# Two-layer hybrid encoder on one core: gates' products one stage ahead, strips and paired values in the recurrence, the logarithm's guard on VectorE

## The chip, the cores and the metric

One core of one Trainium2 chip runs the whole kernel. The metric is device time in microseconds of one launch, of which three runs are shown; a profile of one further execution goes with them. Engines: TensorE (PE; its weight loads are a row of their own, PEld), VectorE (DVE), ScalarE (ACT), GpSimd (POOL), and SyncE (SP), which issues all transfers here.

## What is computed

Batch 1, 512 tokens, width 1024, two layers, float32. Each layer adds three gated branches, then cross-attention over 256 memory tokens, then a SwiGLU of width 2816:

```python
h = _rmsnorm(x, g_mix[l])
(a_cq, a_ckv, a_kr, b_q, b_ff, b_fb, b_i, b_g,
 c_q, c_k, c_v, gate_a, gate_b, gate_c) = _split_cols(h @ w_in[l], IN_SPLITS)
y_a = _mla(...)          # latent attention, 8 heads
y_b = _hgrn2(...)        # bidirectional gated recurrence, 8 heads, 128 keys, 64 values
y_c = _window_gqa(...)   # attention within 128 tokens, 8 heads
merged = (sigmoid(gate_a) * (y_a @ w_br_a[l]) + sigmoid(gate_b) * (y_b @ w_br_b[l])
          + sigmoid(gate_c) * (y_c @ w_br_c[l]))
x = x + merged @ w_out[l]
x = x + _cross(_rmsnorm(x, g_x[l]), _rmsnorm(mem, g_mem[l]), ...)
x = x + _swiglu(_rmsnorm(x, g_ffn[l]), ...)
```

In the recurrence each direction has a forget gate f per key and token, `log f = log(max(f, TINY))`, decayed queries and keys, and a state; forward and backward outputs of a head are added.

## The kernel before, in words

Activations lie transposed, 128 features by 512 tokens a tile. Products of weights are made of float32r parts: every weight tile is split into a high part (ScalarE, L120) and a low part (VectorE, L121), and `mm3` issues three matmuls (high by high, high by low, low by high). Weights come as one stream of 764 units of 128x512, fetched by SP (L112) into five buffers, split three units ahead of their use; a unit is 4 blocks, so 12 matmuls of 512 columns. Operands that aren't split go to TensorE as plain float32 through `mm` (L151, which is the line of nearly all matmuls).

A layer goes through the recurrence (`hgrn`), latent attention (`mla`), windowed attention (`window`), the end of the merge, the output projection, cross-attention and the feed-forward part. A scheduler puts each engine's instructions into an order when the program is built; the Python order sets priorities. In `mla` and `window`, work of other branches is put between their steps as "fillers": the gates' products (`gates`, L513: 8 chunks of 128 features, 24 matmuls each), their sigmoid, which stays in a buffer, and the branch's output product (`out`, L525), two chunks of gates and then the two products they gate. Branch B fills `mla`, branch A fills `window`, and branch C mostly follows after it.

In `hgrn` the decay of head i+2 (`hgrn_decay`) is worked out while head i is at its scores. The decay takes the logarithm in two pieces, since the table's range doesn't hold it in one: f clamped from above by KNEE and below by TINY on GpSimd (L404), f clamped from below on VectorE (L405), two logarithms (L406, L407), and their sum on GpSimd (L408); then scans (L411 and on), the decayed queries and keys (L438, L439), and their level tables `lt` (L457). `hgrn_scores` makes a 512x512 matrix of scores of one head as 4x4 blocks of 128 tokens (keys on the partitions). The diagonal blocks come in pieces: a full 128x128 product forward into bank `bd` and one backward into bank `bb` (L469, L470), and over them 64x64 and 32x32 products from the level tables (L472 to L478). A mask selects (`copy_predicated`, L482), the two are added (L484) and split (L487, L488). The off-diagonal blocks fill three more banks (L490 to L502), each split too (L504). The values of one head are 4 x 3 matmuls of 128 columns by 512 (L367), of which 64 rows are kept. Values themselves are turned by `vturn` (L280) and split.

Of the kernel before, what the change touches and what calls it, by code (L numbers as in the profile page):

```python
# [48 lines left out]
def _consts():  # L49
# [21 lines left out]
    mb = same & (p[:, None] >= p[None, :])  # L71
# [4 lines left out]
class _K:  # L76
# [119 lines left out]
    def setup(self):  # L196
# [25 lines left out]
        self.zz = self.tl("zz", [P, 2, 4, P])  # L222
        nc.gpsimd.memset(self.zz, 0.0)
# [66 lines left out]
    def hgrn(self, l, x, xg, acc):  # L290
# [13 lines left out]
        def take_z(hd, zs):  # L304
# [27 lines left out]
        take_z(heads[1], [proj("f", 1), proj("b", 1)])  # L332
# [3 lines left out]
        a = self.hgrn_scores(heads[0])  # L336
        decay(heads[1])
        y = self.pairs4(4)
        for i in range(8):
            pr = i // 2  # L340
            if i > 0:
                a = self.hgrn_scores(heads[i])
            if i % 2 == 0:
                osb = self.t2()
                if 0 < i < 6:
                    values(pr + 1)
            else:
# [6 lines left out]
            if i < 6:  # L354
                take_z(heads[i + 2], [proj("f", i + 2), proj("b", i + 2)])
# [7 lines left out]
            ob = self.bank()  # L363
            vh, vl = vs[pr]
            for j in range(4):
                s = slice(j * T, (j + 1) * T)
                self.mm3(ob, (vh[:, j], vl[:, j]), (a[0][:, s], a[1][:, s]), j == 0, j == 3)  # L367
            hf = slice(64 * (i % 2), 64 * (i % 2) + 64)
            nc.scalar.activation(osb[hf], ob[hf], AF.Copy)
            if i % 2 == 1:  # L370
                sq = self.t2()
# [22 lines left out]
    def hgrn_decay(self, l, hd, d):  # L394
# [9 lines left out]
        nc.gpsimd.tensor_scalar(g, f, TINY, KNEE, op0=ALU.max, op1=ALU.min)  # L404
# [55 lines left out]
    def hgrn_scores(self, hd):  # L460
# [5 lines left out]
        bd, bb = self.bank([P, 4, P]), self.bank([P, 4, P])  # L466
        for j in range(4):
            js = slice(j * P, (j + 1) * P)
            one(bd[:, j], qk[:, 1, js], qk[:, 0, js])  # L469
            one(bb[:, j], qk[:, 3, js], qk[:, 2, js])  # L470
        for j in range(4):
            one(bd[0:64, j, 64:128], lf[:, 1, 1, 64 * j:64 * j + 64], lf[:, 1, 0, 64 * j:64 * j + 64])  # L472
            one(bd[64:128, j, 0:64], lr[:, 1, 1, 64 * j:64 * j + 64], lr[:, 1, 0, 64 * j:64 * j + 64])
            for i in range(2):
                a, b = 64 * i, 64 * i + 32
                ps = slice(64 * j + 32 * i, 64 * j + 32 * i + 32)
# [685 lines left out]
```

## Time and profile before

| | us |
|---|---|
| runs | 2447.57, 2450.2, 2451.07 (median 2450.2) |
| profiled execution, its own time | 2445.72 |
| its span (first to last instruction) | 2443.9 |
| TensorE busy, matmuls / weight loads | 2396.9 / 1966.2 |
| VectorE / ScalarE / GpSimd busy | 1503.9 / 1194.2 / 262.9 |
| bytes moved | 220.96 MB, 90 GB/s over the span |

Busy time of TensorE is that of matmuls that overlap one another; a float32 matmul stands as two records. A stage's idle time of TensorE is its length less its busy time. Times are us from the first instruction.

### The profile page before, as it was taken

To read this page: it belongs to the slowest core of one execution; us is meant where nothing else is said; L and a number is where in the kernel's file an instruction comes from. 1 tells how busy PE (TensorE), PEld (TensorE's weight loads), DVE (VectorE), ACT (ScalarE), POOL (GpSimd) and SP (SyncE) were. 2 spreads that over 40 slices of the span, in tenths; PEclk is the share of its full clock that TensorE was granted. 3 is DMA by queue.
4 is the path that set the end of the run, shared out by engine and by line. 5 is a ranking of instruction groups with operands and counts; after the bars stand their busy time and mean duration, and the time that the engine had idled before them with its cause. 6 is when DMAs were issued, how large, how long until landed. Compare 5 with 4: busy or idle time off the path is not lost.

```text
span 2443.9 us, 32499 instructions
## 1 busy us (share of the span) xinstructions
PE 2396.9 (98%) x11974; PEld 1966.2 (80%) x11974; DVE 1503.9 (62%) x2745; ACT 1194.2 (49%) x2169; POOL 262.9 (11%) x197
## 2 busy tenths in 40 slices
PE   8999999999999999999998999999999999999998
PEld 6788877788888888888877887877888888888886
DVE  8877766665565655355577786666656566553553
ACT  7666665555444533233466665654544444332332
POOL 2455300000000000000035452000000000000000
PEclk9999999999999999999999999999999999999999
DMA  4212222123442333333421212212324522333332
GB/s 141 61 57 70 82 70 66 62 82 107 151 139 86 91 96 95 99 95 99 127 77 61 70 61 74 74 57 71 90 84 148 147 87 82 96 95 99 96 98 75
DMA packets 119681, 220.96 MB, mean 90 GB/s; under 512 B 13281, under 2 KB 15585, under 8 KB 119137
## 3 DMA queue, kind: packets, MB, share of 16 engines
q1 hardware_dynamic: 119520, 218.88, 29.8%
q8 instruction: 94, 1.54, 0.3%
q14 instruction: 67, 0.54, 0.1%
HBM read 214.63 MB, written 4.19 MB: 90 GB/s over the span
## 4 chain that ended last, share of the span: by engine, by line
PE 85%; DVE 8%; ACT 3%; POOL 2%; issue 1%; DMA 1%; SPq 0%; DVEq 0%; ACTq 0%; POOLq 0%
PE ps L151 83%; POOL t L404 2%; DVE c L457 1%; PE ps L643 1%; DVE smx L411 1%; PE ps L784 1%; POOL t L408 1%; DVE c L439 1%; DVE t L411 1%; DVE wlo L121 1%; DVE c L181 0%; ACT whi L120 0%; DVE c L438 0%; DVE zz L482 0%; DMA c<-in_memT_dram 0%
## 5 line engine op out<-in xcount | busy, mean ns | idle before, releaser
L151 PE MATMUL ps<-c,whi 128*128 128x512 f32 (+1 forms) x5696 | 1734.7, 387 | 6.5 <-ACT whi L120 6.2
L151 PEld LDWEIGHTS ps<-c,whi 128*128 128x128 f32 x5696 | 1059.4, 188 | 232.8 <-issue 10.4
L151 PE MATMUL ps<-c,wlo 128*128 128x512 f32 (+1 forms) x2848 | 1098.4, 386 | 15.3 <-DVE wlo L121 15.2
L120 ACT ACTIVATE whi<-wraw 128x512 fp32r<-128x512 f32 x764 | 475.3, 630 | 858.1 <-PE ps L151 626.3
L121 DVE TENSOR_TENSOR wlo<-wraw,whi 128x512 fp32r<-128x512 f32 x764 | 521.0, 690 | 552.9 <-ACT whi L120 539.8
L151 PEld LDWEIGHTS ps<-c,wlo 128*128 128x128 f32 x2848 | 536.1, 188 | 127.3 <-DVE wlo L121 20.5
L151 PE MATMUL ps<-c,t 128*128 128x512 f32 (+6 forms) x1024 | 188.0, 393 | 4.0 <-DVE c L181 3.7
L404 POOL TENSOR_SCALAR t<-t 128x512 f32<-128x512 f32 x32 | 71.8, 2244 | 1067.4 <-ACT t L401 1065.9
L151 PEld LDWEIGHTS ps<-c,t 128*128 128x128 f32 (+2 forms) x1024 | 127.8, 176 | 48.0 <-issue 20.2
L457 POOL TENSOR_TENSOR c<-c,smx 128x256 f32<-128x256 f32 x128 | 144.9, 1161 | 73.8 <-DVE c L438 61.4
L982 DVE TENSOR_TENSOR t<-ps,t 128x512 f32<-128x512 f32 x112 | 76.3, 688 | 103.0 <-PE ps L151 103.0
L151 PE MATMUL ps<-c 128*32 128x32 f32 (+3 forms) x1280 | 110.6, 259 | 5.5 <-DVE c L439 5.5
L151 PEld LDWEIGHTS ps<-c 128*32 128x32 f32 (+2 forms) x1280 | 96.8, 151 | 21.9 <-DVE c L439 4.0
L181 DVE TENSOR_TENSOR c<-ps,c 128x512 fp32r<-128x512 f32 (+2 forms) x126 | 80.2, 650 | 23.7 <-ACT c L180 23.4
L180 ACT ACTIVATE c<-ps 128x512 fp32r<-128x512 f32 (+2 forms) x126 | 68.4, 565 | 43.9 <-PE ps L151 42.6
L964 DVE TENSOR_TENSOR c<-ps,c 128x512 f32<-128x512 f32 x64 | 44.2, 691 | 72.8 <-PE ps L151 72.8
L457 DVE TENSOR_TENSOR c<-c,smx 128x256 f32<-128x256 f32 x128 | 67.7, 587 | 0.3
L408 POOL TENSOR_TENSOR t<-t,t 128x512 f32<-128x512 f32 x32 | 45.1, 1409 | 86.7 <-ACT t L407 86.7
L181 DVE TENSOR_TENSOR c<-t,c 128x512 fp32r<-128x512 f32 (+1 forms) x84 | 51.9, 632 | 2.9 <-ACT c L180 2.9
L180 ACT ACTIVATE c<-t 128x512 fp32r<-128x512 f32 (+1 forms) x84 | 48.0, 581 | 9.7 <-DVE t L390 3.3
L406 ACT ACTIVATE t<-t 128x512 f32<-128x512 f32 x32 | 20.1, 630 | 62.5 <-POOL t L404 62.5
L411 DVE TENSOR_TENSOR_SCAN t<-cst,t 128x512 f32<-128x512 f32 x32 | 40.8, 1275 | 15.8 <-POOL t L408 15.8
(145 smaller groups left out, 1830.6 us busy)
## 6 DMA issues: line engine op xcount, KB each, us to landing
wraw<-in_w_dram SPq DMA_DIRECT2D x764, 256.0 KB, 2.6
c<-in_xT_dram SPq DMA_DIRECT2D x16, 256.0 KB, 5.2
t<-in_bias_dram SPq DMA_DIRECT2D x16, 192.0 KB, 3.0
c<-in_memT_dram SPq DMA_DIRECT2D x3, 1024.0 KB, 8.1
xs<-c SPq DMA_DIRECT2D x8, 256.0 KB, 2.4
c<-xs SPq DMA_DIRECT2D x8, 256.0 KB, 5.3
out_dram<-t SPq DMA_DIRECT2D x8, 256.0 KB, 2.1
t<-in_rope_dram SPq DMA_DIRECT2D x4, 256.0 KB, 3.4
```

The source lines that it names most:

```text
L120: self.nc.scalar.activation(hi, raw, AF.Copy)
L121: self.nc.vector.tensor_tensor(lo, raw, hi.bitcast(F32), op=ALU.subtract)
L151: self.nc.tensor.matmul(o, a, b, start=start, stop=stop)
L180: nc.scalar.activation(hi, src, AF.Copy)
L181: nc.vector.tensor_tensor(lo, src, hi.bitcast(F32), op=ALU.subtract)
L404: nc.gpsimd.tensor_scalar(g, f, TINY, KNEE, op0=ALU.max, op1=ALU.min)
L408: nc.gpsimd.tensor_tensor(f, f, g, op=ALU.add)
L411: scan = lambda o, m, x: nc.vector.tensor_tensor_scan(o, m, x, 0.0, op0=ALU.mult, op1=ALU.add)
L439: nc.vector.scalar_tensor_tensor(ki, kk, omlb, cc, op0=ALU.mult, op1=ALU.mult)
L457: eng.tensor_tensor(ov, sv, ev, op=ALU.mult)
L964: nc.vector.tensor_tensor(x[c], b, xold[c], op=ALU.add)
L982: self.nc.vector.tensor_tensor(t, b, r, op=ALU.mult)
```

## The change

Four things. The gates' products: sigmoids are now stored to device memory (`gate_put`) and loaded again by `out`. The chunks of branch B are made in the recurrence, two at its entry (as four banks at once with head 1's decay inputs) and one ahead of each of heads 2 to 7; those of branch A fill `mla` beside branch B's output products; those of branch C fill `window` beside branch A's, two of them and branch C's output products follow after. The strips: a diagonal block's pieces are now all 32 columns of the array wide, four at a time, and the backward piece is only the four 32x32 blocks of the diagonal; bank `bb` shrinks to a quarter. The values: scores and values stay plain float32, and both heads of a pair go into one bank, 64 columns each. The guard: the clamp with TINY and KNEE is on VectorE. The rest of the kernel stands as it was.

```diff
-    mb = same & (p[:, None] >= p[None, :])
+    mb = (p[:, None] % 32) >= p[None, :]
...
 def vturn(self, vf):
-        v = (self.t2(F32R, (P, 4, P)), self.t2(F32R, (P, 4, P)))
-        self.split(v[0], v[1], tb)
+        v = self.t2(shape=(P, 4, P))
+        nc.scalar.activation(v, tb, AF.Copy)
...
 def hgrn(self, l, x, xg, acc, sd):
-        def take_z(hd, zs):
+        def take_z(hd, zs, gs=()):
+            for c, b in gs:
+                self.gate_put(sd, c, b)
...
-        take_z(heads[1], [proj("f", 1), proj("b", 1)])
+        g0, g1, b0, b1 = self.projs("w_in", l, np.arange(D), [O_GB + ar, O_GB + P + ar, off["f"] + P + ar,
+                                                             off["b"] + P + ar], h)
+        take_z(heads[1], [b0, b1], [(0, g0), (1, g1)])
...
+            gs = [(i + 2, self.gate_proj(l, O_GB, i + 2, h))] if i < 6 else []
...
-                take_z(heads[i + 2], [proj("f", i + 2), proj("b", i + 2)])
+                take_z(heads[i + 2], [proj("f", i + 2), proj("b", i + 2)], gs)
...
-            ob = self.bank()
-            vh, vl = vs[pr]
-            for j in range(4):
-                s = slice(j * T, (j + 1) * T)
-                self.mm3(ob, (vh[:, j], vl[:, j]), (a[0][:, s], a[1][:, s]), j == 0, j == 3)
-            hf = slice(64 * (i % 2), 64 * (i % 2) + 64)
-            nc.scalar.activation(osb[hf], ob[hf], AF.Copy)
             if i % 2 == 1:
+                ob = self.bank()
+                for j in range(4):
+                    for e in range(2):
+                        hf = slice(64 * e, 64 * e + 64)
+                        self.mm(ob[hf], vs[pr][:, j, hf], heads[i - 1 + e]["a"][:, j * T:(j + 1) * T], j == 0, j == 3)
...
 def hgrn_decay(self, l, hd, d):
-        nc.gpsimd.tensor_scalar(g, f, TINY, KNEE, op0=ALU.max, op1=ALU.min)
+        nc.vector.tensor_scalar(g, f, TINY, KNEE, op0=ALU.max, op1=ALU.min)
...
 def hgrn_scores(self, hd):
-        for j in range(4):
-            one(bd[:, j], qk[:, 1, js], qk[:, 0, js])
-            one(bb[:, j], qk[:, 3, js], qk[:, 2, js])
+            for g in range(4):
+                one(bd[q4[g], j, q4[g]], qk[:, 1, js[g]], qk[:, 0, js[g]])
+            for g in range(4):
+                one(bb[q4[g], j], qk[:, 3, js[g]], qk[:, 2, js[g]])
+            for g in range(4):
+                one(bd[q4[g], j, q4[g ^ 1]], lt[:, 0, 1, ps], lt[:, 0, 0, ps])
+            for g in range(4):
+                one(bd[q4[g], j, cs], lt[:, 1, 1, ks], lt[:, 1, 0, 64 * j:64 * j + 64])
...
+        nc.vector.copy_predicated(self.zz, self.msk[:, 0].unsqueeze(1).to_broadcast([P, 4, P]), bd)
+        nc.vector.copy_predicated(self.zb, self.msk[:, 1, 0:32].unsqueeze(1).to_broadcast([P, 4, 32]), bb)
+        nc.scalar.activation(dg, self.zz, AF.Copy)
+        for g in range(4):
+            tt(dg[q4[g], :, q4[g]], self.zz[q4[g], :, q4[g]], self.zb[q4[g]], op=ALU.add)
...
-            self.split(ah[:, s], al[:, s], g)
+            nc.scalar.activation(a[:, i * 640 + 128:(i + 1) * 640], g, AF.Copy)
...
+    def gate_put(self, sd, c, b):
+        sg = self.t2()
+        last = self.nc.scalar.activation(sg, b, AF.Sigmoid)
+        self.nc.sync.dma_start(sd[:, c], sg)
+        return last
...
 def branch(self, l, sd, wname, rows, y, merged, first):
+        def out(c):
             def run():
+                sg = self.t2()
+                nc.sync.dma_start(sg, sd[:, c])
+                pb = self.projs(wname, l, rows, [c * P + np.arange(P)], y)[0]
...
 def layers(self):
+            sd, gs = self.gates(l, O_GA, h)
+            for c in range(0, KC, 2):
+                self.fillers += gs[c:c + 2] + [both(br[c], br[c + 1])]
...
+            sd, gs = self.gates(l, O_GC, h)
+            for c in range(6):
+                self.fillers += [gs[c], br[c]]
+            self.fillers += br[6:]
...
-            for i, f in enumerate(brc):
+            for i, f in enumerate(gs[6:] + self.branch(l, sd, "w_br_c", crow, yc, merged, False)):
```

What moves is seen in the built programs. TensorE, the scores of head 1 of the first layer, before (`ps_927` is bank `bd`, `ps_928` is `bb`; `c_131` holds the decayed queries and keys, `c_135` and `c_139` the two level tables; sizes are rows written by columns):

```order
L151 MATMUL ps_927<-c_131_653 128x128
L151 MATMUL ps_928<-c_131_653 128x128
L151 MATMUL ps_927<-c_135_676 64x64
L151 MATMUL ps_927<-c_139_707 64x64
L151 MATMUL ps_927<-c_135_676 32x32
L151 MATMUL ps_927<-c_139_707 32x32
L151 MATMUL ps_927<-c_135_676 32x32
L151 MATMUL ps_927<-c_139_707 32x32
```

and now (`ps_1058` is `bd`, `ps_1059` is `bb`):

```order
L151 MATMUL ps_1058<-c_144_761 32x32 x4
L151 MATMUL ps_1059<-c_144_761 32x32 x4
L151 MATMUL ps_1058<-c_148_784 32x32
L151 MATMUL ps_1058<-c_152_815 32x32
L151 MATMUL ps_1058<-c_148_784 32x32
L151 MATMUL ps_1058<-c_152_815 32x32
L151 MATMUL ps_1058<-c_148_784 32x64 x2
L151 MATMUL ps_1058<-c_152_815 32x64 x2
```

Before, eight full products come first and then four times a group of 64 and a group of 32; now four times the eight rows shown, with no product of another width between the first and the last.

VectorE at the end of the first layer's merge, around the norm of the memory tokens (L264, now L265, and its splits L181 of 256 columns), before (`wlo_6147` is the low part of the output projection's fourth unit; L533, L534 are branch C's last products, L964 the residual's first add):

```order
L264 SCALAR_TENSOR_TENSOR t_1285_6109<-c_1277_6085,small_64,rmem_5692 128x256
L264 SCALAR_TENSOR_TENSOR t_1286_6113<-c_1277_6085,small_64,rmem_5692 128x256
L181 TENSOR_TENSOR c_1274_6058<-c_566_2967,c_1273_6057 128x512
L181 TENSOR_TENSOR c_1279_6088<-t_1285_6109,c_1278_6087 128x256
L181 TENSOR_TENSOR c_1279_6088<-t_1286_6113,c_1278_6087 128x256
L264 SCALAR_TENSOR_TENSOR t_1287_6117<-c_1277_6085,small_64,rmem_5692 128x256
L121 TENSOR_TENSOR wlo_6147<-wraw_6035,whi_6146 128x512
L181 TENSOR_TENSOR c_1279_6088<-t_1287_6117,c_1278_6087 128x256
L964 TENSOR_TENSOR c_1275_6075<-ps_6125,c_1275_6075 128x512
L121 TENSOR_TENSOR wlo_6171<-wraw_6126,whi_6170 128x512
```

and now (`wlo_6459` is the low part of the projection's eighth unit, L970 the residual's adds):

```order
L181 TENSOR_TENSOR c_1279_6315<-t_1283_6328,c_1278_6314 128x256
L181 TENSOR_TENSOR c_1279_6315<-t_1284_6332,c_1278_6314 128x256
L181 TENSOR_TENSOR c_1279_6315<-t_1285_6336,c_1278_6314 128x256
L265 SCALAR_TENSOR_TENSOR t_1286_6340<-c_1277_6312,small_64,rmem_6052 128x256
L265 SCALAR_TENSOR_TENSOR t_1287_6344<-c_1277_6312,small_64,rmem_6052 128x256
L956 SCALAR_TENSOR_TENSOR c_1289_6349<-c_1275_6302,small_64,c_1288_6348 128x512
L181 TENSOR_TENSOR c_1279_6315<-t_1286_6340,c_1278_6314 128x256
L181 TENSOR_TENSOR c_1279_6315<-t_1287_6344,c_1278_6314 128x256
L970 TENSOR_TENSOR c_1275_6302<-ps_6394,c_1275_6302 128x512
L121 TENSOR_TENSOR wlo_6459<-wraw_6413,whi_6458 128x512
```

The norm's rows, eight and eight with their splits, stood between the low parts of the projection's third and fourth units, mixed with branch C's last products; now they stand in one block between those of its seventh and eighth units, behind the residual's first add.

SP's queue, in the windowed attention of the first layer, before (L747 loads the bias tables):

```order
L112 DMA wraw_4607<-in_w_dram 128x512
L747 DMA t_915_4420<-in_bias_dram 128x384
L747 DMA t_921_4427<-in_bias_dram 128x384
L112 DMA wraw_4625<-in_w_dram 128x512
L112 DMA wraw_4644<-in_w_dram 128x512
L112 DMA wraw_4665<-in_w_dram 128x512
```

and now (L536 stores a gate, L546 loads one, L753 the bias tables):

```order
L536 DMA gate_7584_4916<-t_1015_5161 128x512
L112 DMA wraw_5303<-in_w_dram 128x512
L112 DMA wraw_5321<-in_w_dram 128x512
L112 DMA wraw_5359<-in_w_dram 128x512
L112 DMA wraw_5377<-in_w_dram 128x512
L536 DMA gate_7584_4916<-t_1016_5164 128x512
L112 DMA wraw_5398<-in_w_dram 128x512
L753 DMA t_1024_5190<-in_bias_dram 128x384
L753 DMA t_1030_5197<-in_bias_dram 128x384
L546 DMA t_1045_5279<-gate_5536_3441 128x512
L546 DMA t_1069_5395<-gate_5536_3441 128x512
```

Stores and loads of gates stand between the weights' fetches, where only these and the bias tables stood.

## Rows read from the trace of the kernel before

**Rows 1.** Busy time by stage: start:end, length, then busy us (records) of each engine.

```profile
58.00:117.00 59.00, 54.92 (x320) 45.10 (x320) 49.59 (x91) 35.77 (x61) 31.39 (x27) 0.89 0.17 50
183.00:248.00 65.00, 63.81 (x383) 52.51 (x383) 50.92 (x96) 41.37 (x72) 32.78 (x24) 1.00 0.22 66
477.00:594.00 117.00, 117.00 (x640) 93.61 (x639) 71.46 (x193) 62.45 (x146) 0.00 (x0) 1.00 0.29 89
1230.00:1327.00 97.00, 87.51 (x480) 71.67 (x479) 82.14 (x147) 64.54 (x108) 46.52 (x36) 0.98 0.19 58
```

The columns after the length are PE, PEld, DVE, ACT, POOL, the granted clock of TensorE, the DMA engines' share and GB/s.

**Rows 2.** TensorE's waits, whole run: releaser, us in total, times, longest.

```profile
PE ps L151 <- DVE wlo L121: 15.2, 10, 3.7
...
PE ps L151 <- DVE c L439: 5.5, 2, 3.8
PE ps L151 <- DVE c L181: 4.0, 3, 1.9
```

**Rows 3.** Busy time by window, one head's scores in the recurrence.

```profile
190.75:192.63 1.88, 1.88 (x17) 1.75 (x15) 0.81 (x2) 1.47 (x3) 0.32 (x1) 1.00 0.65 173
192.63:194.49 1.85, 1.85 (x49) 1.42 (x49) 0.88 (x1) 0.00 (x0) 1.77 (x2) 1.00 0.31 110
194.49:197.13 2.65, 2.65 (x25) 2.44 (x17) 0.91 (x4) 0.55 (x2) 2.06 (x1) 1.00 0.00 0
```

A record that runs on from the window before is counted in both.

**Rows 4.** Busy time by window: a group of 64x64, then one of 32x32.

```profile
192.63:192.90 0.27, 0.27 (x5) 0.20 (x4) 0.00 (x0) 0.00 (x0) 0.27 (x1) 1.00 0.87 301
192.90:193.09 0.20, 0.20 (x12) 0.16 (x8) 0.00 (x0) 0.00 (x0) 0.20 (x1) 1.00 0.94 362
```

Four and eight records start in these two.

**Rows 5.** Groups by shape: values of latent attention. Busy us, mean ns, idle before.

```profile
L151 PE MATMUL ps<-c,t 128*64 128x512 f32 x128 | 29.2, 598 | 0.0
```

**Rows 6.** TensorE in order of time, around the values of two heads: start, us.

```profile
215.01 2.88 PE L151 MATMUL ps<-c,t 128*128 128x512 f32 x12
217.73 0.62 PE L151 MATMUL ps<-c,whi 128*128 128x512 f32 x2
...
246.42 3.19 PE L151 MATMUL ps<-c,t 128*128 128x512 f32 x12
249.45 0.62 PE L151 MATMUL ps<-c,whi 128*128 128x512 f32 x2
```

**Rows 7.** Groups by shape: VectorE and GpSimd.

```profile
L482 DVE COPY_PREDICATED zz<-msk,ps 128x512 f32<-128x512 int32 x32 | 23.3, 738 | 5.2 <-PE ps L151 5.2
L488 DVE TENSOR_TENSOR c<-t,c 128x512 fp32r<-128x512 f32 x16 | 13.3, 833 | 1.4 <-ACT c L487 1.4
L181 DVE TENSOR_TENSOR c<-ps,c 128x512 fp32r<-128x512 f32 x90 | 59.8, 684 | 22.8 <-ACT c L180 22.8
L425 DVE TENSOR_TENSOR smx<-smx,t 128x64 f32<-128x64 f32 x32 | 8.6, 269 | 0.2
L405 DVE TENSOR_SCALAR t<-t 128x512 f32<-128x512 f32 x32 | 13.6, 424 | 25.8 <-POOL t L404 25.8
L404 POOL TENSOR_SCALAR t<-t 128x512 f32<-128x512 f32 x32 | 71.8, 2244 | 1067.4 <-ACT t L401 1065.9
L264 DVE SCALAR_TENSOR_TENSOR t<-c,small,rmem 128x256 f32<-128x256 f32 x16 | 7.0, 479 | 2.0 <-DMA c<-in_memT_dram 2.0
L181 DVE TENSOR_TENSOR c<-t,c 128x256 fp32r<-128x256 f32 x16 | 6.4, 418 | 0.0
```

**Rows 8.** Busy time by window, two stretches at a lower granted clock (third from last).

```profile
56.90:67.10 10.20, 9.44 (x72) 8.04 (x73) 9.35 (x15) 4.79 (x9) 4.49 (x5) 0.50 0.39 123
...
111.50:114.90 3.40, 3.40 (x9) 2.15 (x7) 3.37 (x6) 3.39 (x7) 3.06 (x4) 0.50 0.28 77
```

**Rows 9.** SP's longest wait in total, and the weights' fetches (size, median us to landing).

```profile
SPq L112 <- DVE wlo L121: 1955.4, 699, 21.1
...
wraw<-in_w_dram SPq DMA_DIRECT2D x764, 256.0 KB, 2.6
```

More of the change, by code (lines that the diff above doesn't have):

```diff
@@ L335, in hgrn @@
         values(1)
-        a = self.hgrn_scores(heads[0])
+        self.hgrn_scores(heads[0])
         decay(heads[1])
@@ L502, in hgrn_scores, with gates, chunk @@
                 one(g[:, 384:512], lr[:, 2, 1, h1], lr[:, 2, 0, h1])
-            s = slice(i * 640 + 128, (i + 1) * 640)
-            self.split(ah[:, s], al[:, s], g)
-        return ah, al
-    def branch(self, l, gate, wname, rows, y, h, merged, first):
-        nc = self.nc
-        allr = np.arange(D)
-        st = {}
-        def gates(c):
+            nc.scalar.activation(a[:, i * 640 + 128:(i + 1) * 640], g, AF.Copy)
+        hd["a"] = a
+    def gates(self, l, gate, h):
+        sd = self.dr.tile([P, KC, T], F32, name=f"gate{l}_{gate}")
+        st = []
+        def chunk(c):
             def run():
-                st[c] = self.projs("w_in", l, allr, [gate + c * P + np.arange(P)], h)[0]
+                st.append(self.gate_proj(l, gate, c, h))
                 if c % 2 == 1:
                     for i in (c - 1, c):
-                        sg = self.t2()
-                        last = nc.scalar.activation(sg, st[i], AF.Sigmoid)
-                        st[i] = sg
+                        last = self.gate_put(sd, i, st.pop(0))
                     if c == KC - 1 and gate == O_GC:
@@ L523, in gates, with gate_proj, branch @@
             return run
[L525 to L539 removed]
+        return sd, [chunk(c) for c in range(KC)]
+    def gate_proj(self, l, gate, c, h):
+        return self.projs("w_in", l, np.arange(D), [gate + c * P + np.arange(P)], h)[0]
+    def gate_put(self, sd, c, b):
[3 more added lines that the diff above has]
+        return last
+    def branch(self, l, sd, wname, rows, y, merged, first):
+        nc = self.nc
+        def out(c):
+            def run():
+                sg = self.t2()
+                nc.sync.dma_start(sg, sd[:, c])
+                pb = self.projs(wname, l, rows, [c * P + np.arange(P)], y)[0]
+                if first:
+                    nc.vector.tensor_tensor(merged[c], pb, sg, op=ALU.mult)
+                else:
+                    nc.vector.tensor_tensor(sg, pb, sg, op=ALU.mult)
+                    nc.vector.tensor_tensor(merged[c], merged[c], sg, op=ALU.add)
+            return run
+        return [out(c) for c in range(KC)]
     def mla_pre(self, l, h):
@@ L648, in turned @@
             return pt
-        def vtoken(vf):
-            tb = self.bank([P, 4, P])
-            for j in range(4):
-                nc.tensor.transpose(tb[:, j], vf[:, j * P:(j + 1) * P], self.ident)
-            v = self.t2(shape=(P, 4, P))
-            nc.scalar.activation(v, tb, AF.Copy)
-            return v
         def values(pr, v, pts):
@@ L1087, in layers, with both, run @@
         assert self.pos == UNIT and self.unit == NUNIT - 1, (self.unit, self.pos, len(self.rec))
+def both(f, g):
+    def run():
+        f()
+        g()
+    return run
 def _t5_bucket(rel):
```

71 lines of the change are left out of this document (24 added, 47 removed).

## Prediction

> **What bounds the kernel now.** I read the table by stage first, then TensorE's waits, then single windows of one head of the recurrence. In the table by stage [rows 1] the reader compares the length of a stage with TensorE's busy time. In the windowed attention (477 to 594 us) it is busy all 117.00 us, in one pair of heads of the recurrence (183 to 248) 63.81 of 65.00, and VectorE, the next, 50.92. So TensorE's own work sets the time nearly everywhere, and a us of it that goes is a us of the kernel. Only at the two entries of the recurrence (58 to 117, 1230 to 1327) does it stand still for 4.1 and 9.5 us. What it waits for there is in its waits [rows 2]: the low parts of the weights (L121), the keys of a head's decay (L439), the low parts of the scores (L181). The chain of waits runs through GpSimd and VectorE in this stage, but these are chains that end only a little after TensorE has run out of work; I weigh them by TensorE's waits, not by their length.
>
> **Strips.** One head's scores take three windows [rows 3]: 16 full 128x128 records in 1.88 us, 48 narrow records in 1.85 us, and the off-diagonal blocks in 2.65 us, which stay. (A program's float32 matmul is two records.) The change replaces the first two by 16 groups of four strips 32 columns wide: 12 groups with 32 moving columns, 4 with 64. What does a group cost? The full records give 1.88/16/128 = 0.92 ns per moving column. By that a group of four 32-column strips, first halves side by side and then second halves, streams for 2 x 32 x 0.92 = 0.06 us, and a 64-wide pair for 2 x 64 x 0.92 = 0.12. Measured [rows 4]: a 64-wide group 0.27, the 32-wide group of eight records behind it 0.20. Each carries 0.14 to 0.15 us that no streaming explains. In the kernel before, every one of these groups follows a group of another width (64, 32, 64, 32). Equal widths in succession stand in the latent attention's values: 128 records of 64 x 512 in 29.2 us [rows 5], two at a time, so 0.456 us a step against 512 x 0.92 = 0.47 streamed: no such addition. I take it that the 0.15 us belongs to the change of width. Then 16 groups of one width cost 12 x 0.06 + 4 x 0.12 = 1.2 us, and 0.15 on entering and on leaving: 1.5 where 3.73 stood. That saves 2.2 to 2.3 us a head, **-36 us** over 16 heads. Bounds: 2.5 us a head (-40) without the two changes of width; if every group keeps its addition, 12 x 0.20 + 4 x 0.27 = 3.5, and 0.2 a head (-4).
>
> The Trainium skill's page "TensorEngine Tiling (Array Packing)", section Key Properties, says that changing the tiling mode, and not just the tile, drains the engine. That is the reading taken here; by it the sum is the -36.
>
> **Values of a pair at once.** Before, 12 matmuls per head on split operands: 2.72 us from the start of the twelve to the next row, and 3.03 for the other head of the pair [rows 6], 5.75 a pair. Now 8 float32 matmuls, 64 wide, both heads side by side: the shape of the latent attention's values, 16 records, 29.2/8 = 3.65 us [rows 5], and 0.1 to 0.3 for two changes of width. Per pair 1.8 to 2.0, over 8 pairs **-15 us**. Bounds: -17 without the changes of width; if the halves did not run side by side, 7.3 us and +12, which rows 5 speak against.
>
> **VectorE and GpSimd.** Off VectorE go, per head [rows 7]: one of two wide predicated copies (0.738), the wide sum of the two diagonals (L484, not counted), the split of the diagonal (0.833) and three splits of blocks (3 x 0.684): 3.6 us. On it come a predicated copy of a quarter the width and four adds of 32 partitions, five of 0.27 (L425, 64 columns) to 0.42 (L405, wider), say 1.7, and the guard twice, which as one more clamp of the same shape costs 0.424 (L405) where GpSimd took 2.244. Net -1.0 us a head or better, and two dependent steps of 2.2 us leave GpSimd's chain. None of it lies on TensorE's path while that is busy: no term, but it bears on the waits.
>
> **Gates one stage ahead.** The products are the same, only their place changes; 12 matmuls are a unit of weights, 2.72 us [rows 6], so a gate chunk is 5.4 us. One now stands ahead of each head's recurrence, so a pair of 65 us grows by 10.9 and shrinks by 2 x 2.25 + 1.9 = 6.4, to some 69, with VectorE's 50.9 changed by about +0.7 for four more units less the 2 x 1.0. The decay thus gets more cover, not less. Two chunks also stand at the entry, with head 1's decay inputs as four banks at once, 8 units, 21.8 us where 10.9 stood ahead of the same scores. The wait for L439 (5.5 in two) was a first head's scores waiting for its decay; 10.9 us more cover it. The wait for L181 (4.0, the longest 1.9) was values waiting right behind their scores; they now stand a gate, two products and more later. I take **-9 us** for both. The clock: from the end of the longest wait (L439, 3.8) on, 10.2 us ran at a granted clock of 0.50, the 1.2 GHz level, and 3.4 more ahead of the first head's values [rows 8], both after TensorE had stood still. Half of 10.2 is lost there; I take **-5** and nothing for the other. The waits for L121 (15.2, ten) come from VectorE's queue: low parts of weights stand behind the recurrence's work. With less of that I take half, **-7**.
>
> **What the gates' way through memory costs.** 48 stores and 48 loads of 256 KB join SP's queue: 25 MB to 221 MB. SP waits 1955 us for slots that L121 frees [rows 9]: it runs ahead and has time. A store waits for ScalarE's sigmoid, and behind it stand the weights' fetches. By the order of the changed kernel at least 8 units are fetched beyond the gate's own at every store: 8 x 2.72 = 21.8 us of TensorE's work, against 2.6 us for a fetch to land. I cost the stores at nothing; that lead hides them. The last stage is where cover is thin: the third branch's eight products now follow each other, 21.8 us, in which VectorE has 8 products, 8 adds, 8 splits and 9 low parts, 33 x 0.68 = 22 us, and then the memory tokens' norm, 8 x 0.479 + 8 x 0.418 = 7.2 us [rows 7], in one block ahead of the next low part. That low part is of the projection's eighth unit: TensorE needs it 7 x 2.72 = 19 us into the projection, and VectorE, which starts the block when the first product is through (5.4 us) and a little more, gives it at some 16. I cost it at nothing, with 3 us of cover; without that cover it would be a wait of the block's 7 us in each layer. For waits that I don't see I add **+3**.
>
> **Sum.** -36 - 15 - 9 - 5 - 7 + 3 = -69 against the profiled execution's own 2445.7 us, so 2377 there. The median of the runs, 2450.2, is 4.5 above it: 2381.
>
> **Rivals.** (a) Small matmuls are bound by their number. A head's 128 strip records would each take their turn. For it: eight records took 0.20 us in rows 4, 25 ns each. Against it: the group of 64 columns with half as many records took longer, 0.27, so it isn't the number that is paid for. Price: 128 x 25 ns to 3.5, so 3.2 to 3.5 us a head in place of 1.5, 16 x 1.7 to 2.0 = 27 to 32 us given back: about 2411. The same skill page, section Instruction Overhead, says that each matmul has about 60 cycles of overhead and that a tiling factor should not be taken from a dimension that is already small, which is this rival.
> (b) Slower: the gates' loads come late. VectorE takes its queue in order, so a product that waits for a load holds the low parts behind it, and TensorE with them. Three units are split ahead, 8.2 us; from a load that comes that late on, TensorE stands. A load waits in SP's queue for a buffer of the 25 and for the stores ahead of it. At 2 us at each of the 48 loads: +96, so 2477. Against it: the loads stand some eight units ahead of their use, and weights land in 2.6 us.
> (c) Nothing gained: the recurrence turns out to be bound by its decay chain, and the saved work comes back as waits. For it: the chain of waits passes through GpSimd and VectorE there. Against it: a pair's TensorE time grows to about 69 us while VectorE keeps near 50. Price: the 69 us come back, about 2450.
>
> **How the numbers follow.** Forecast 0.83, (a) 0.09, (b) 0.04, (c) 0.04. The forecast's own range: all bounds in favour, -40 - 17 - 9 - 10 - 15, is 2359; without the 21 us from waits and clock it is 2402. To hold 8 in 10 I go a little into (a): 2360 to 2412. A measurement of this kernel tells 0.2%, 5 us, from no change. Faster by more: the forecast and (a), with a little of (c), 0.93; the rest of (c) is no change, 0.03; (b) is slower, 0.04.
>
> **What would show it.** Right: a head's strips (first strip to first off-diagonal block) in about 1.5 us; 16 records of 64 x 512 per pair in 3.6 to 3.9; no wait of TensorE for a decay at the entries, and no half clock behind it; a pair of the recurrence near 69 us with TensorE idle in it for under 1 us. Wrong: strips at 0.2 us a group (a); TensorE's waits led by VectorE's products that wait for a DMA (b); TensorE's idle time in the recurrence grown by tens of us (c).

## The result, and the profile after

The changed kernel takes 2371.44 us (median of four runs, 2370.55 to 2372.48) beside 2450.59 for the kernel before on the same chip: a ratio of 0.968, 95% interval 0.9663 to 0.9696, 79.2 us less. The forecast was 2381 within 2360 to 2412, faster. The profiled execution took 2371.25 us, its span is 2369.5.

The first part of the page: busy us of each engine.

```profile
PE 2336.9 (99%) x12934; PEld 1901.6 (80%) x12934; DVE 1469.8 (62%) x2753; ACT 1187.3 (50%) x2162; POOL 167.8 (7%) x165
```

TensorE is busy 60.0 us less than before, and of the 74.4 us by which the span is shorter the other 14.4 are idle time of TensorE: 32.6 us now, 47.0 before. Busy time by stage, for the same four places as [rows 1]: first entry of the recurrence, one pair of its heads, windowed attention, second entry.

```profile
58.00:117.00 59.00, 58.02 (x510) 47.97 (x509) 48.98 (x98) 44.35 (x76) 22.75 (x23) 1.00 0.27 82
217.30:286.70 69.40, 67.15 (x546) 53.20 (x545) 48.98 (x102) 42.93 (x75) 19.16 (x17) 1.00 0.30 92
481.00:598.00 117.00, 114.92 (x634) 90.57 (x633) 73.82 (x199) 67.83 (x155) 0.00 (x0) 1.00 0.38 123
1193.00:1290.00 97.00, 97.00 (x683) 80.70 (x683) 83.78 (x159) 70.09 (x118) 31.02 (x30) 1.00 0.29 86
```

Read three things in it. At the entries TensorE is now busy nearly throughout, and the granted clock is 1.00 where it was 0.89 and 0.98. A pair takes 69.4 us, as forecast, but in 2.25 of them TensorE is idle. And the windowed attention, which had no idle time, has 2.1 us. TensorE's waits, whole run (releaser, us, times, longest), against [rows 2]:

```profile
PE ps L151 <- DVE wlo L121: 6.5, 4, 2.3
...
PE ps L151 <- DVE smw L767: 2.3, 2, 1.3
...
PE ps L151 <- ACT t L183: 2.0, 2, 1.0
```

The waits for decays (L439) and for low parts of scores (L181) are gone, those for low parts of weights (L121) fell from 15.2 to 6.5. New are L767 and L183, both in the windowed attention.

One head's scores by window, strips and then off-diagonal blocks ([rows 3] were 1.88, 1.85 and 2.65), and the groups of strips and of 64 x 512 values by shape:

```profile
196.51:197.92 1.41, 1.41 (x129) 1.32 (x128) 0.78 (x3) 1.29 (x3) 0.00 (x0) 1.00 0.11 17
197.92:200.56 2.64, 2.64 (x20) 2.43 (x17) 1.53 (x3) 0.00 (x0) 1.27 (x1) 1.00 0.37 96
```

```profile
L151 PE MATMUL ps<-c 128*32 128x32 f32 x1536 | 22.1, 197 | 0.0
L151 PE MATMUL ps<-c 128*32 128x64 f32 x512 | 20.9, 223 | 0.2
L151 PE MATMUL ps<-c,t 128*64 128x512 f32 x256 | 58.5, 598 | 0.0
```

The 128 strip records take 1.41 us, where 1.5 were forecast. Of the 256 records of values half are the recurrence's: 29.3 us for eight pairs, 3.66 a pair, as forecast.

The largest wait left in the recurrence stands once a layer. VectorE's low parts of weights and TensorE there (start, us; in brackets the idle time ahead and its releaser):

```profile
196.19 0.69 DVE L121 TENSOR_TENSOR wlo<-wraw,whi 128x512 fp32r<-128x512 f32 x1 [1.69 <-ACT whi L120]
...
209.75 0.67 DVE L121 TENSOR_TENSOR wlo<-wraw,whi 128x512 fp32r<-128x512 f32 x1
...
219.14 3.10 DVE L121 TENSOR_TENSOR wlo<-wraw,whi 128x512 fp32r<-128x512 f32 x5
```

```profile
219.89 0.50 PE L151 MATMUL ps<-c,wlo 128*128 128x512 f32 x1 [2.25 <-DVE wlo L121]
```

Between 196.9 and 219.1 us VectorE makes one low part; everything else in these 22 us is one head's decay, the masks and the sums, and the output of the pair before (L395, L396, L181). Meanwhile TensorE lives on what was split ahead, its **lead** (five buffers, each good for 2.72 us), and on products that take no weights. How many low parts lie in such a **run** of VectorE, and how long it is, turned out to be what several parts of this change act on together.

### The profile page after: what moved, and what is told of

Same layout as the page of the kernel before. It is cut to its first block, busy times and chain, and to the rows that moved or that the text cites. A ratio compares the mean times of both kernels' runs of the same rounds, so it can differ in the third digit from the quotient of the medians.

```text
span 2369.5 us, 34666 instructions
## 1 busy us (share of the span) xinstructions
PE 2336.9 (99%) x12934; PEld 1901.6 (80%) x12934; DVE 1469.8 (62%) x2753; ACT 1187.3 (50%) x2162; POOL 167.8 (7%) x165
## 4 chain that ended last, share of the span: by engine, by line
PE 85%; DVE 6%; issue 4%; POOL 2%; ACT 2%; DMA 1%; POOLq 0%; DVEq 0%; SPq 0%; ACTq 0%
PE ps L151 83%; POOL c L463 1%; PE ps L658 1%; DVE c L463 1%; DVE t L417 1%; POOL t L414 1%; DVE wlo L121 1%; DVE c L444 1%; PE ps L790 1%; DVE c L445 0%; ACT whi L120 0%; PE ps L939 0%; DMA t<-in_bias_dram 0%; DMA wraw<-in_w_dram 0%; PE ps L286 0%
## 5 line engine op out<-in xcount | busy, mean ns | idle before, releaser
L121 DVE TENSOR_TENSOR wlo<-wraw,whi 128x512 fp32r<-128x512 f32 x764 | 526.5, 697 | 545.7 <-ACT whi L120 535.9
L151 PE MATMUL ps<-c,t 128*64 128x512 f32 (+6 forms) x960 | 167.5, 418 | 4.5 <-DVE smw L767 2.3
L151 PEld LDWEIGHTS ps<-c,t 128*64 128x64 f32 (+2 forms) x960 | 99.7, 167 | 55.3 <-issue 31.6
L463 POOL TENSOR_TENSOR c<-c,smx 128x256 f32<-128x256 f32 x128 | 122.8, 988 | 111.0 <-DVE c L444 82.8
L970 DVE TENSOR_TENSOR c<-ps,c 128x512 f32<-128x512 f32 x64 | 44.2, 690 | 70.1 <-PE ps L151 70.1
L463 DVE TENSOR_TENSOR c<-c,smx 128x256 f32<-128x256 f32 x128 | 81.6, 695 | 0.2
L151 PEld LDWEIGHTS ps<-c 128*32 128x32 f32 (+1 forms) x2304 | 61.2, 120 | 12.2 <-PE ps L151 5.3
L151 PE MATMUL ps<-c 128*32 128x32 f32 (+3 forms) x2304 | 69.3, 218 | 0.2
L180 ACT ACTIVATE c<-ps 128x512 fp32r<-128x512 f32 (+2 forms) x78 | 42.7, 547 | 39.9 <-PE ps L151 38.9
L181 DVE TENSOR_TENSOR c<-ps,c 128x512 fp32r<-128x512 f32 (+2 forms) x78 | 49.3, 632 | 20.8 <-ACT c L180 20.4
L181 DVE TENSOR_TENSOR c<-t,c 128x512 fp32r<-128x512 f32 (+1 forms) x84 | 51.6, 634 | 3.3 <-ACT c L180 3.3
L645 ACT ACTIVATE t<-ps,sm 128x512 f32<-128x512 f32 x64 | 43.5, 687 | 12.6 <-DVE sm L643 12.5
```

The costliest lines, as they stand in the source:

```text
L121: self.nc.vector.tensor_tensor(lo, raw, hi.bitcast(F32), op=ALU.subtract)
L151: self.nc.tensor.matmul(o, a, b, start=start, stop=stop)
L180: nc.scalar.activation(hi, src, AF.Copy)
L181: nc.vector.tensor_tensor(lo, src, hi.bitcast(F32), op=ALU.subtract)
L463: eng.tensor_tensor(ov, sv, ev, op=ALU.mult)
L645: nc.scalar.activation(p, s, AF.Exp, bias=nm, accum_out=sm)
```

## The experiments

No kernel here leaves out any of the work. Times are compared with the changed kernel, at 2371.4 us, or at 2372.6 where it ran beside them (gates, guard on GpSimd, stores); ratios are to the kernel before, run beside each.

**The strips, taken back out** (old pieces, masks and sum, over scores that stay unsplit).

```diff
-            for g in range(4):
-                one(bd[q4[g], j, q4[g]], qk[:, 1, js[g]], qk[:, 0, js[g]])
...
+            one(bd[:, j], qk[:, 1, js], qk[:, 0, js])
+            one(bb[:, j], qk[:, 3, js], qk[:, 2, js])
```

> The changed kernel with the old diagonal blocks alone: full 128x128 products into two banks, 64x64 and 32x32 pieces over them, two masked copies 512 wide and one wide sum. My theory (the time goes with TensorE's work, and a head's strips take 1.46 us where the old pieces took 3.73): 16 x 2.25 = +36 us, so about 2407; the first head's scores may wait a little more. Rival (small matmuls bound by their number, so the strips were worth little and the gain came from waits and clock): +4 to +9 us, about 2378.

Measured: 2398.88 us, +27.4 (ratio to before 0.9793, 0.9774 to 0.9811). The page:

```profile
PE 2370.7 (99%) x11910; PEld 1934.7 (81%) x11910; DVE 1458.4 (61%) x2705; ACT 1182.3 (49%) x2146; POOL 181.1 (8%) x165
```

TensorE's busy time rises by 33.8 us, near the 36 expected, but its idle time falls by 6.6 (span 2396.7): the waits for L121 are gone altogether. So the strips' work is worth nearly what was forecast, and 6.6 us of it stand in the changed kernel as waits. Two things can have ended these waits, and this run alone doesn't tell them apart: TensorE has more work to wait behind, and VectorE is busy 11.4 us less (1458.4 for 1469.8; the strips' narrow adds cost it more than the old wide steps). The next two settle it. The rival of the records' number is out.

**Widths mixed** within the strips, and **strip by strip**, the same products in another order.

```diff
...
-            for g in range(4):
...
-                one(bd[q4[g], j, cs], lt[:, 1, 1, ks], lt[:, 1, 0, 64 * j:64 * j + 64])
+            ks = slice(64 * j, 64 * j + 64)
+            one(bd[0:64, j, 64:128], lf[:, 1, 1, ks], lf[:, 1, 0, ks])
+            one(bd[64:128, j, 0:64], lr[:, 1, 1, ks], lr[:, 1, 0, ks])
```

> The changed kernel with one edit in the strips: at each of the four diagonal blocks the pieces from the first level table are two 64x64 products in place of four of 32x64, so that the array's tiling changes from 32 to 64 and back four times in a head, with 16 records fewer. My theory (a change of width costs some 0.1 to 0.15 us and the number of records nothing): 8 changes more in a head less the one at the end that is there already, 7 to 8 x 0.10 to 0.15 x 16 heads = +11 to +19 us, about 2386. Rival (number of records): 128 to 112 records of 11 to 25 ns, -3 to -6 us, about 2367.

```diff
-        for j in range(4):
-            js = [slice(j * P + 32 * g, j * P + 32 * g + 32) for g in range(4)]
-            for g in range(4):
...
+        for g in range(4):
+            for j in range(4):
+                js = slice(j * P + 32 * g, j * P + 32 * g + 32)
```

> The same strips in another order: all products of the first strip, then all of the second, and so on, so that neighbours in the queue share a strip of the array and can't run side by side. My theory (four strips run side by side, and streaming is what costs: 0.92 ns a moving column): 128 records x 32 to 64 columns, 48 x 2 x 32 x 0.92 ns + 16 x 2 x 64 x 0.92 ns = 2.8 + 1.9 = 4.7 us a head instead of 1.46, 16 x 3.2 = +52 us, about 2423. Rival (each record takes its turn at 11 ns whatever its place): no change, 2371.

Measured: 2381.18 (+9.7; 0.972, 0.9699 to 0.9741) and 2412.94 (+41.5; 0.9849, 0.9831 to 0.9866). One head's diagonal pieces by window, of the first and of the second kernel:

```profile
199.05:201.41 2.36, 2.36 (x114) 1.93 (x113) 0.90 (x3) 1.28 (x3) 0.91 (x1) 1.00 0.29 77
```

```profile
207.43:211.93 4.50, 4.50 (x130) 4.41 (x129) 2.34 (x5) 1.46 (x4) 1.27 (x1) 1.00 0.25 62
```

Seven changes of width more (four from 32 to 64, three back) cost 2.36 - 1.41 = 0.95 us a head, 0.136 each, with 16 records fewer. And records of one strip in succession take 4.50/128 = 35 ns each, where neighbours on four strips take 1.41/128 = 11. Both cost less time than TensorE's steps say (16 x 0.95 = 15.2, 16 x 3.09 = 49). TensorE is busy 14.0 and 47.6 us longer, and idle 4.4 and 6.0 us less: its waits for L121, 6.5 us in the changed kernel, are 2.3 in the first and none in the second. VectorE's work is the same in both (busy 1471.0 and 1470.0), and the low parts stand at nearly the same places in its run, so it is TensorE's longer work that uses up the waits.

**Values by head** (scores and values split again, 12 products a head).

```diff
+            for j in range(4):
+                s = slice(j * T, (j + 1) * T)
+                self.mm3(ob, (vh[:, j], vl[:, j]), (ah[:, s], al[:, s]), j == 0, j == 3)
...
-            nc.scalar.activation(a[:, i * 640 + 128:(i + 1) * 640], g, AF.Copy)
...
+            self.split(ah[:, s], al[:, s], g)
```

> The changed kernel with the old values alone: scores and values split into two parts, and 12 products of 128 columns a head, right behind the head's scores. My theory: 5.75 us of TensorE a pair where 3.66 stand, 8 x 2.1 = +17 us, and the wait of the values for the low parts of the scores back (L181 before, up to 4 us); VectorE gets 4 splits a head (4 x 0.7 = 2.8 us), which may show as up to 3 us of waits: +17 to +24, about 2391. Rival (TensorE's time there is covered by VectorE's chain): 0 to +4 us, about 2373.

Measured: 2454.36, +82.9 (1.0021, 1.0009 to 1.0032): the whole gain is gone. TensorE waits

```profile
PE ps L151 <- DVE wlo L121: 46.2, 10, 8.9
```

and VectorE's rows show why: in one head of a pair the run, now with the splits (L181, L511) in it, has no low part at all in 22 us.

```profile
177.30 0.69 DVE L121 TENSOR_TENSOR wlo<-wraw,whi 128x512 fp32r<-128x512 f32 x1 [2.03 <-PE ps L296]
...
200.19 1.88 DVE L121 TENSOR_TENSOR wlo<-wraw,whi 128x512 fp32r<-128x512 f32 x3
```

From its start to the group behind it this run is as long as the changed kernel's (177.30 to 200.19 here, 22.89 us; 196.19 to 219.14 there, 22.95); what is gone is the low part in its middle. The splits had been counted as 3 us of waits; this version brought 40 for low parts, and TensorE's busy time rises by 36.2 us where 16.7 of work were added (mean granted clock 0.988 for 0.999).

**Gates at their old places.**

```diff
-        take_z(heads[1], [b0, b1], [(0, g0), (1, g1)])
+        take_z(heads[1], [proj("f", 1), proj("b", 1)])
...
-            gs = [(i + 2, self.gate_proj(l, O_GB, i + 2, h))] if i < 6 else []
```

> The changed kernel with the gates' products at their old places (branch B's in the latent attention, A's in the windowed attention, C's after it), sigmoids kept in buffers, no way through memory. My theory: TensorE's work is the same, but at the two entries of the recurrence the first head's scores wait for their decay again (5.5 us before) and the clock falls to 0.50 behind it (10 us in all before), and waits for low parts of weights come back (15 us before, 6.5 now), less the 2 us of the new waits in the windowed attention: +12 to +25 us, about 2389. Rival (strips and values took the load off the decay's chain, the gates' place is worth nothing): 0 to +4 us; if the way through memory costs something of its own, below 0.

Measured: 2417.23, +44.7 (0.9879, 0.986 to 0.9897). TensorE's waits:

```profile
PE ps L151 <- DVE c L440: 12.5, 4, 4.8
PE ps L151 <- DVE c L491: 11.9, 4, 3.6
```

L440 is the decays' keys (L445 in the changed kernel), awaited by the first heads' scores, as expected, and twice as long as in the kernel before; L491 is the sums of the scores' diagonal (L496), awaited by the values, which come a gate's product sooner. These and smaller ones make 24.3 us more idle time. With the same work TensorE is also busy 20.9 us longer (2357.8); the lower mean clock (0.993 for 0.999, over 2415 us) is some 14 of that by estimate, the rest is not explained. So the cost is about twice the 12 to 25 expected. The gates' chunks cover both chains; the waits for low parts hardly change (7.1 us for 6.5).

**Guard on GpSimd.**

```diff
-        nc.vector.tensor_scalar(g, f, TINY, KNEE, op0=ALU.max, op1=ALU.min)
+        nc.gpsimd.tensor_scalar(g, f, TINY, KNEE, op0=ALU.max, op1=ALU.min)
```

> The changed kernel with the logarithm's guard back on GpSimd (one line). My theory: the decay has cover nearly everywhere, only the first head's at the two entries is near the path, where 2 x 1.8 us of chain come back: 0 to +7 us, about 2374. Rival (VectorE is the one that is short, its backlog makes the remaining waits for low parts of weights): 0 to -5 us, about 2369. Third: GpSimd's chain grows back on every head and TensorE waits for decays: +20 us or more.

Measured: 2415.17, +42.6 (0.9875, 0.9856 to 0.9895). That is the third case by its size but not by its cause: TensorE waits 37.6 us for low parts (L121), and none for decays. VectorE's run at the place of the wait, TensorE's step, and the clock behind it (window, busy, granted clock):

```profile
206.98 0.69 DVE L121 TENSOR_TENSOR wlo<-wraw,whi 128x512 fp32r<-128x512 f32 x1 [2.02 <-ACT whi L120]
...
210.06 1.23 DVE L417 TENSOR_TENSOR_SCAN t<-cst,t 128x512 f32<-128x512 f32 x1 [2.05 <-POOL t L414]
213.03 0.43 DVE L411 TENSOR_SCALAR t<-t 128x512 f32<-128x512 f32 x1 [1.74 <-POOL t L410]
...
230.45 3.10 DVE L121 TENSOR_TENSOR wlo<-wraw,whi 128x512 fp32r<-128x512 f32 x5
```

```profile
231.19 0.79 PE L151 MATMUL ps<-c,wlo 128*128 128x512 f32 x1 [5.50 <-DVE wlo L121]
```

```profile
231.20:235.30 4.10, 4.10 (x10) 3.23 (x11) 2.35 (x4) 0.51 (x1) 0.00 (x0) 0.50 0.61 158
```

VectorE now stands 1.74 us for the guard (L410, on GpSimd), and the run holds no low part from 207.7 to 230.5. TensorE waits 5.50 us, and then goes on at a clock of 0.50, the 1.2 GHz level, up to 235.3. Over the whole execution that makes 31.6 us more idle time (64.2) and 12.0 us more busy time. Here too the run is about as long as in the changed kernel (206.98 to 230.45, 23.5 us for 22.95), and the low part that stood in its middle (209.75) is out of it, since the program's order is made anew for the one line; the two effects of the line, the waiting and the order, I did not separate.

**Stores of gates on ScalarE's queue.** In the changed kernel SP's rows ahead of the windowed attention's first scores, and what VectorE waits for:

```profile
509.82 0.33 SPq L536 DMA_DIRECT2D gate<-t  x1
510.24 0.38 SPq L112 DMA_DIRECT2D wraw<-in_w_dram  x1
510.67 0.92 SPq L753 DMA_DIRECT2D t<-in_bias_dram  x2
```

```profile
513.78 0.48 DVE L767 CUSTOM_DVE_ANT_0 t<-ps,t,small 128x256 f32<-128x256 f32 x1 [2.13 <-DMA t<-in_bias_dram]
```

```diff
-        self.nc.sync.dma_start(sd[:, c], sg)
+        self.nc.scalar.dma_start(sd[:, c], sg)
```

> The changed kernel with the gates' stores issued by ScalarE's queue in place of SyncE's (one line). My theory: in the windowed attention a store that waits for a sigmoid holds the loads of the bias tables behind it, and TensorE waits 1.0 us for a score with bias and up to 1.0 us for a split in each layer; these waits go: -2 to -4 us, about 2368. Rival (the waits come from VectorE's order): 0. Third: the issue of 48 stores takes ScalarE's time on high parts of weights: 0 to +3 us.

> The changed kernel itself, as the level for the three runs beside it on the same chip: 2371.4, within 0.1%.

Measured: 2374.10 (2373.58 to 2376.33) beside 2372.58 (2371.81 to 2374.49) for the changed kernel: no gain. The wait is still there (VectorE stands 2.26 us for the bias tables; TensorE's waits for L767 and L183 are 1.8 and 2.5 us, 4.3 together as before), and SP's rows show what holds the tables: six fetches of weights that wait for buffers.

```profile
499.77 13.55 SPq L112 DMA_DIRECT2D wraw<-in_w_dram  x6
513.37 0.97 SPq L753 DMA_DIRECT2D t<-in_bias_dram  x2
```

My theory of the store falls; the tables come late because they stand behind weights' fetches.

**Guard alone, and strips alone, on the kernel before** (the same edits as above, the other way round; the strips' scores are split as before).

> The kernel before with the guard alone moved to VectorE (one line). Taken back out of the changed kernel, this line cost 43 us. My theory: in the recurrence TensorE waits only where VectorE's run of decay work is longer than the split weights ahead of it last; in the kernel before that excess is 0.9 us a pair of heads (1.6 us steps of TensorE at 145.9, 211.1 and 276.0), so only this, 6 x 0.9 = 5 us, and some of the waits at the entries can be won: -5 to -15 us, about 2440. Rival (the guard is worth its 43 us in any surroundings): about 2406. Third (VectorE has no room): 0 to +5.

> The kernel before with the strips alone. My theory: TensorE's work falls by 16 x 2.25 = 36 us, but in the kernel before TensorE already waits once a pair for low parts of weights that stand behind the decays in VectorE's queue, and less work of TensorE between them lengthens that wait: of the 36 us only 0 to 12 come, about 2443. Rival (parts add up: what TensorE no longer does is won): -36, about 2414.

Measured beside 2448.51 for the kernel before: the guard 2442.24, -6.3 (0.9978, 0.9968 to 0.9988), and the strips 2497.87, **+49.4** (1.0196, 1.0176 to 1.0216). The first is as expected: the waits for L121, 15.2 us, are down to

```profile
PE ps L151 <- DVE wlo L121: 1.9, 1, 1.9
```

with the chains at the entries longer in their place (L439 9.8, L181 10.3; TensorE's idle time is 44.7 us for 47.0). The second is worse than anything expected. TensorE's waits with strips alone, VectorE's low parts there, and the clock behind a wait:

```profile
PE ps L151 <- DVE wlo L121: 78.1, 14, 9.0
```

```profile
165.69 0.69 DVE L121 TENSOR_TENSOR wlo<-wraw,whi 128x512 fp32r<-128x512 f32 x1 [2.02 <-PE ps L286]
190.50 3.08 DVE L121 TENSOR_TENSOR wlo<-wraw,whi 128x512 fp32r<-128x512 f32 x5
...
204.05 0.69 DVE L121 TENSOR_TENSOR wlo<-wraw,whi 128x512 fp32r<-128x512 f32 x1 [1.88 <-ACT whi L120]
...
226.91 0.99 DVE L121 TENSOR_TENSOR wlo<-wraw,whi 128x512 fp32r<-128x512 f32 x1
```

```profile
190.00:193.40 3.40, 2.18 (x5) 1.79 (x6) 3.40 (x6) 0.14 (x1) 0.00 (x0) 0.50 0.28 86
```

The same rows of the kernel before:

```profile
158.76 0.69 DVE L121 TENSOR_TENSOR wlo<-wraw,whi 128x512 fp32r<-128x512 f32 x1 [0.73 <-PE ps L285]
...
174.95 0.68 DVE L121 TENSOR_TENSOR wlo<-wraw,whi 128x512 fp32r<-128x512 f32 x1
182.86 3.08 DVE L121 TENSOR_TENSOR wlo<-wraw,whi 128x512 fp32r<-128x512 f32 x5
...
190.53 0.69 DVE L121 TENSOR_TENSOR wlo<-wraw,whi 128x512 fp32r<-128x512 f32 x1 [0.83 <-ACT whi L120]
211.86 0.68 DVE L121 TENSOR_TENSOR wlo<-wraw,whi 128x512 fp32r<-128x512 f32 x1
```

```profile
212.59 0.50 PE L151 MATMUL ps<-c,wlo 128*128 128x512 f32 x1 [1.16 <-DVE wlo L121]
```

Before, the stretches without a low part took 16.2 and 21.3 us; with strips alone 24.8 and 22.9, while TensorE reaches the end of its split weights 2.3 us a head sooner. The two differ. In the first, the work up to the group of five took 24.1 us before (158.76 to 182.86) and takes 24.8 now; what has changed most is that the low part in its middle has left, by the order of the queue, and TensorE waits 7.22 us behind it (191.22). In the second the order is the old one with three narrow adds of the strips put in: the stretch grows by 1.5 us, TensorE's cover shrinks by 2.3 (3.73 less 1.41), together 3.8, and TensorE's wait grows from 1.16 (212.59) to 5.18 us (227.96), by 4.0. TensorE stands still for 64.6 us more (111.6 against 47.0), and of the 36 us of work that it saves only 12.4 show in its busy time (2384.5), since it also runs at a clock of 0.50 behind the waits (mean granted clock 0.978 for 0.994).

**One buffer of split weights more**, in the changed kernel and with the guard on GpSimd. If length of run against lead is what decides, one more unit of lead, 2.72 us, must cut each wait.

```diff
-NT2 = 25
-WB = 5
+NT2 = 24
+WB = 6
...
-        raw = self.tl("wraw", [P, UNIT * P], F32, WB)
+        raw = self.tl("wraw", [P, UNIT * P], F32, 4)
```

> The changed kernel with six buffers of split weights in place of five (four of fetched ones in place of five and one temporary fewer, to make room). My theory: the waits for low parts that are left (2.2 us at 219.9 and its like in the second layer, 6.5 us in all) are those of VectorE's run against five units of lead; one more unit is 2.72 us: they go, -4 to -7 us, about 2366. Rival (the fetched weights or the temporaries become short, or the order that comes out is another): 0 to +10.

> Guard on GpSimd and six buffers of split weights in the changed kernel. My theory (the 43 us of the guard on GpSimd are waits of 5 to 6 us against the lead, and a lower clock behind them): 2.72 us more of lead leaves waits of about 3 us at six places and less of the low clock: 10 to 25 us above the changed kernel, about 2388. Rival (the decays' chain sets the pace, lead changes nothing): 2415.

Measured: 2366.42 (2365.05 to 2367.16; 0.9661, 0.9643 to 0.9679), 5.0 us below the changed kernel, the lowest time here; the two ratios' intervals overlap, and the firmer sign is TensorE's idle time, 28.5 us for 32.6. And 2392.61 (+21.2; 0.977, 0.9751 to 0.9788), so half of what the guard on GpSimd cost comes back. Waits for low parts, first of one and then of the other:

```profile
PE ps L151 <- DVE wlo L121: 1.0, 2, 0.8
```

```profile
PE ps L151 <- DVE wlo L121: 14.8, 8, 2.8
```

VectorE's low parts in the first of the two, around the place where the changed kernel waits 2.25 us:

```profile
198.06 0.69 DVE L121 TENSOR_TENSOR wlo<-wraw,whi 128x512 fp32r<-128x512 f32 x1 [0.87 <-ACT whi L120]
...
211.62 0.67 DVE L121 TENSOR_TENSOR wlo<-wraw,whi 128x512 fp32r<-128x512 f32 x1
...
221.01 2.49 DVE L121 TENSOR_TENSOR wlo<-wraw,whi 128x512 fp32r<-128x512 f32 x4
```

The run is the changed kernel's, row by row in the same order and 22.95 us long in both, and the wait of 2.25 us, less than one unit, is gone. With the guard on GpSimd the order through the run is also kept; at the same place of each layer the waits of 5.50 and 5.23 us become 2.51 and 2.50, 3.0 and 2.7 less, about one unit. The first waits of a layer's recurrence fall less (4.42 and 2.61 to 2.14 both). Two others, 5.64 and 5.62 us behind the third run of a layer, go altogether, which is more than one unit explains, and the longest left (2.77) stands at the first entry, where the waits were 1.34 and less. This is the strongest evidence for the reading, since VectorE's order through these runs stayed as it was while the lead grew.

## Why the prediction was right, and which steps were not

- **Strips, -36.** The size of a head's strips was right (1.41 us against 1.5; 33.8 us of TensorE's busy time when taken back out), and so was its ground: the addition belongs to the change of width (0.136 us measured, 0.15 taken), and strips run side by side. Rival (a) is shown wrong by three experiments. The Trainium skill's page "TensorEngine Tiling (Array Packing)", section Key Properties, says that a change of tiling mode drains the engine, without a price. The trace agrees, with 0.136 us a change.
- **Values, -15.** TensorE's part was right: 3.66 us a pair for 5.75, 16.7 in all. What the old values cost by VectorE's queue was given no term of its own, and is the larger part: taken back out, the new values cost 83 us.
- **Waits L439 and L181, -9.** Both gone, 9.5 us, and waits of the same two kinds (L440, L491) are back when the gates go to their old places.
- **Clock, -5.** Mis-sized: only the first of four stretches was counted. Two are in [rows 8], the other two are at the second entry of the kernel before:

```profile
1319.80:1323.20 3.40, 2.98 (x7) 2.40 (x8) 3.37 (x6) 3.37 (x6) 2.17 (x3) 0.50 0.23 77
1326.60:1330.00 3.40, 3.40 (x9) 2.67 (x9) 3.40 (x7) 3.37 (x6) 0.00 (x0) 0.51 0.25 55
```

TensorE was busy 19.2 of the 20.4 us of all four, so some 9.6 were lost. In the profiled execution no stretch at 0.50 is left in the recurrence, and they came back.
- **Waits L121, -7.** 8.7 us. But "TensorE idle for under 1 us" in a pair was wrong at one place in each layer, 2.25 us.
- **Unseen waits, +3.** 4.3 us: the bias tables' (L767, 2.3) and ScalarE's split beside it (L183, 2.0). The first comes from SP's queue, as rival (b) had it, but from the tables' place behind the fetches, and not from the gates' loads: VectorE waited 3.7 us in all for those (L549), and none of TensorE's waits is for what came of them. L183 is not SP's: that split ran on ScalarE right behind a gate's sigmoid (L535) and two copies (L793), from 510.32 us on; no run separates what delayed it.
- **Frame.** 4.5 us were added to come from the profiled execution to the median of the runs; the changed kernel's profiled execution lies at its median (2371.25 and 2371.44). That, and 5.5 us by which the terms fell short (74.5 against 69), make up, within 0.4 us of rounding, the 9.6 between 2381 and 2371.4.
- **The step that failed without showing in the sum** is "none of it lies on TensorE's path while that is busy: no term", on VectorE and GpSimd, and with it "a us of TensorE's work that goes is a us of the kernel". The reason given against rival (c), 69 us of TensorE against 50 of VectorE in a pair, compares sums over a pair, and rival (b) took the lead as three units, where the rows show low parts in groups of five. What decides is how long VectorE goes without a low part against the weights that lie split ahead and TensorE's other work in that time. By that measure the kernel before had no room: its strips alone lose 49 us, which is rival (c) and worse. In the changed kernel each run between 150 and 300 us has a low part inside it; when the values are split again or the guard goes back to GpSimd, one of the two runs of a pair has none; the gates' chunks serve otherwise, as cover for two chains (L440, L491). Taken out one at a time, strips, values, gates and guard cost 27, 83, 45 and 43 us, 198 in sum, where all four together brought 79. So the terms could be added only because the change holds all four. The prediction had no argument for that, and to this extent its total was luck.

Open: every edit lets the scheduler put VectorE's queue into another order. Where the low parts kept their places (widths mixed, strip by strip, six buffers, the second of the stretches with strips alone), TensorE's waits moved the way the work or the lead says. Where they did not (values by head, guard on GpSimd, the first of the stretches with strips alone), the run is nearly as long as it was and has lost its low part, so these numbers hold the part and its order. How much of the 83, the 43 and the 49 us another order would spare was not tried.

## What to carry to other kernels

A bound engine that is fed by another engine's queue has a lead, and what has to be compared with that lead is the longest run of other work in the feeding queue, not the two engines' busy times over a stage. Look at where in that run the feeding work stands, too: with one low part in its middle the run cost 2.25 us of wait here, and without it, 0.5 us longer, 5.50. Work taken off the bound engine shortens its cover, so pair such a saving with a shorter run or a longer lead, and cost the parts of a change by taking each out, since they needn't add up. As measured here, small float32 products go into strips of one width, neighbours on different strips, with as few changes of width as the order allows.

## What had not been expected of the hardware

Whether a wait of 2.25 us is followed by a lower clock differed between two executions of the same kernel at the same place. In the first profile of the changed kernel the clock stayed at 1.00 behind 219.9 us (the pair's row above); in the second:

```profile
221.42 0.58 PE L151 MATMUL ps<-c,wlo 128*128 128x512 f32 x1 [2.25 <-DVE wlo L121]
```

```profile
221.70:225.10 3.40, 3.40 (x9) 2.63 (x9) 2.07 (x4) 1.23 (x3) 0.00 (x0) 0.50 0.78 221
```

Nine matmuls ran in these 3.40 us at 0.50, which at full clock take 0.23 us each (2.72 for twelve, [rows 6]), 2.0 in all: 1.4 us on top of a wait of 2.25. In that same execution the like wait of the second layer, also 2.25 us (1397.71), was followed by a clock of 1.00. Behind the wait of 5.50 us (guard on GpSimd) the clock was at 0.50 as well, for longer, 4.1 us. So a wait here can cost more than its length, by an amount that doesn't come out the same each time.
